# Half of a depthwise conv moved into two MLP blocks, the output projection split by MLP block, and five MLP blocks of 4, 4, 4, 3 and 2 tiles

## The chip, the cores and the metric

The kernel runs on one core of a Trainium2 chip. The metric is the device time of one execution in microseconds (us); three runs of the kernel before gave 2654.08, 2655.58 and 2659.54 us, median 2655.58. Engines: PE is TensorE (matmul; PEld its weight load), DVE is VectorE, ACT is ScalarE, POOL is GpSimd, SP is SyncE, which issues every DMA here. A "tile" of the text is 128 rows of the 17 x 128 = 2176 input rows: tile 0 is the sample rows, tiles 1 to 16 are the prompt.

## The reference, cut to what matters

One layer of an encoder, width 1024, in float32:

```
proj = rmsnorm(x) @ w_in                      # q, k, v, a, g
attn = windowed attention(q, k, v)            # 512 wide; tiles 1..16, and 8 sample batches
u = a * sigmoid(g)                            # 512 channels
c = silu(layernorm(causal depthwise conv of u, 31 taps))
x = x + concat(rmsnorm(attn), rmsnorm(c)) @ w_out
x = x + relu(rmsnorm(x) @ w_up)**2 @ w_down   # 4096 wide
x = x + (p @ w_ple) * sigmoid(rmsnorm(x) @ w_ple_gate);  y = rmsnorm(x)
```

## The kernel before, in words

Every large matmul is done as three, on a high part and a rest of each operand (hi x hi, hi x lo, lo x hi). So each weight of 512 KB is loaded (tile `raw`, 3 buffers), cast on ACT to `w[:, 0]` and its rest taken on POOL to `w[:, 1]` (`weight` and `split`, L117 to L131; weights with a scale take the rest on DVE, L131). There are 8 buffers `w`.

The stages, in order:

- **A**: the columns a and g of `proj`, blocks of 3 tiles; the conv's input goes to `U` (four buffers of 512 prompt rows) and `US` (sample). `conv_block` starts a conv where `CONV_AT` says, 4 tiles at a time. For each of four channel blocks cb it adds 31 taps into an `acc` of 128 x 512: cb 0 to 2 on DVE (L162), cb 3 on POOL (L158) from products of ACT (L157) or POOL (L155). There are 5 buffers `acc`. `conv_post` then does each tile: transposes to PSUM (L168, tile `c`, one buffer), layer norm, back-transposes (L181), swish, store to `M[t]`. Taps have the lowest priority (`LOW`).
- **B**: q, k, v (L266, `mm<-hnb`) and the attention, two or three tiles a block; the result also goes to `M[t]`.
- **C**: `c_tile` loads `M[t]`, splits it and multiplies it with `w_out` (48 matmuls, L533), adds x, and stores `X1[t]`. The eight sample batches are mixed in.
- **MLP**: four blocks of 4, 4, 5 and 4 tiles. A block's normalised, transposed input is `hf` (one buffer; `mlp_front`). The 32 columns f of w_up go in groups of 4: per f 24 matmuls (L266, `up`), then ACT relu and square (L663, L664), DVE `relu<-up,relu` (L665) and the rest `ht<-relu,ht` (L666). After four f come 24 matmuls a tile with w_down (L678, `d`), added to `accf` on DVE (L684). All of w_up and w_down is loaded again for each block.
- **PLE**: the gate with the per-layer embedding, tile by tile.

A scheduler makes each engine's order from priorities and its own idea of time; each engine then runs its list strictly in order. So an instruction that waits holds up all that is behind it on its engine.

Of the kernel before, what the change touches and what calls it, by code (L numbers as in the profile page):

```python
# [72 lines left out]
def build(ctx, tc, nc, a):  # L73
# [64 lines left out]
    cpool = pool(mix, "cpool")
    mixp = ExitStack()
    psc = pool(mixp, "psc", 1, space=PSUM)  # L140

    U = [cpool.tile([P, 4, HALO + 512], F32, name=f"U{i}", bufs=1) for i in range(4)]
    US = cpool.tile([P, 4, DB, HALO + DS], F32, name="US", bufs=1)
    nc.gpsimd.memset(U[0][:, :, 0:HALO], 0.0)

# [18 lines left out]
    def conv_post(accs, off, t):  # L164
        with later(tc, MID):
# [27 lines left out]
            nc.sync.dma_start(M[t][:, 4:8, :], zc)  # L193

    def conv_block(tiles):
        pt = [t for t in tiles if t > 0]
        if 0 in tiles:
            accs = []
            for cb in range(4):
                acc = cpool.tile([P, 512], F32, name="acc", bufs=5)[:, 0:P]  # L200
                accs.append(acc)
                conv_taps(acc.rearrange("p (b s) -> p b s", b=DB),
                          lambda j, cb=cb: US[:, cb, :, j:j + DS], cb,
                          lambda: cpool.tile([P, 512], F32, name="tap")[:, 0:P].rearrange("p (b s) -> p b s", b=DB), 0)
            conv_post(accs, 0, 0)
        if pt:
            n = len(pt) * P
            c0 = (pt[0] - 1) * P
            accs = []
            for cb in range(4):  # L210
                acc = cpool.tile([P, 512], F32, name="acc", bufs=5)
                accs.append(acc)
                conv_taps(acc[:, 0:n], lambda j, cb=cb: U[c0 // 512][:, cb, c0 % 512 + j:c0 % 512 + j + n], cb,
                          lambda: cpool.tile([P, 512], F32, name="tap")[:, 0:n], pt[0])
            for i, t in enumerate(pt):
                conv_post(accs, i * P, t)
# [227 lines left out]
    for bi, tiles in enumerate(B_BLOCKS):  # L444
# [56 lines left out]
        for i in range(nch):  # L501
# [56 lines left out]

    def f_segs(tiles):
        n = len(tiles) * P  # L560
        return [(0, n)] if n <= 512 else [(0, 384), (384, n)]

    def mlp_front(bi, ps, tag, bufs):
        tiles = F_BLOCKS[bi]
        hf = hpool.tile([P, KD, 2, FB * P], F32R, name="hf", align_bytes=ALN)
        hfs[bi] = hf
        xns = []
        for t in tiles:
            xn = hpool.tile([P, D], F32, name="xnf", bufs=XNB)
# [7 lines left out]
    for ti, t in enumerate(C_ORDER[EARLY:]):
        if ti < DB:
            sample_batch(opool, ps2, *samp, ti)
        if ti == DB - 1:  # L580
            nc.sync.dma_start(M[0][:, 0:4, :], samp[2])
        c_tile(t, opool, ps2, opool.tile([P, 8, P], F32, name="mt", bufs=3),
               opool.tile([P, D], F32, name="xc", bufs=3), opool.tile([P, 2, 8, P], F32R, name="ms", bufs=2, align_bytes=ALN),
               opool.tile([P, 8, P], F32, name="sq", bufs=1), dict(bufs=1), dict(bufs=4))
# [56 lines left out]

    for bi, tiles in enumerate(F_BLOCKS):
        segs = f_segs(tiles)
        hf = hfs.pop(bi)
        accs = []
        for t in tiles:
            acc = fpool.tile([P, D], F32, name="accf", bufs=FB)
            nc.sync.dma_start(acc, X1[t])
            accs.append(acc)
        for g in range(NFF // GRP):  # L650
            hts, wds = [], []
            for f in range(g * GRP, (g + 1) * GRP):
                wu = weight(a["w_up"][f].rearrange("p k n -> p (k n)"))
                wd = weight(a["w_down"][f * P:(f + 1) * P, :])
# [3 lines left out]
                for s0, s1 in segs:  # L658
                    w = s1 - s0
                    ps = psf.tile([P, 512], F32, name="up")  # L660
                    proj(ps[:, 0:w], lambda wp, k: wu[:, wp, k * P:(k + 1) * P], lambda k: hf[:, k, :, s0:s1], w)
                    r = fpool.tile([P, 512], F32, name="relu", bufs=2)
                    nc.scalar.activation(r[:, 0:w], ps[:, 0:w], AF.Relu)  # L663
                    nc.scalar.activation(ht[:, 0, s0:s1], r[:, 0:w], AF.Square)  # L664
                    nc.vector.scalar_tensor_tensor(r[:, 0:w], ps[:, 0:w], 0.0, r[:, 0:w], ALU.max, ALU.mult)  # L665
                    nc.vector.tensor_tensor(ht[:, 1, s0:s1], r[:, 0:w], ht[:, 0, s0:s1].bitcast(F32), ALU.subtract)  # L666
            if g == NFF // GRP - 1:
# [20 lines left out]

    def ple_back(t, x2, xg):
        ss = fpool.tile([P, 2], F32, name="gss", bufs=2)  # L690
# [3 lines left out]
        for nh, ns in enumerate((h0, h1)):  # L694
# [119 lines left out]
```

## Time and profile before

| | |
|---|---|
| median of three runs | 2655.58 us |
| profiled execution | 2655.39 us |
| its span, first to last instruction | 2653.6 us |
| mean granted TensorE clock | 0.973 of full speed |
| PE busy | 2526.9 us (95%) |
| DVE busy | 1273.2 us (48%) |
| ACT busy | 978.4 us (37%) |
| POOL busy | 1121.7 us (42%) |
| weight-load DMA of `raw` | 512 KB each, 3.5 us to land |

Read it by stage, not by the totals: stages A and B end at 665 us, the conv's last posts at 689, C at 897, the MLP at 2400, PLE at 2653.6. The 48% of DVE is an average of stages in which it is full and others in which it is a third busy.

### The profile page before, as it was taken

How to read it: one execution, taken by the hardware profiler on the slowest of the kernel's cores; microseconds unless marked ns; L12 is line 12 of the kernel's file. 1: busy time of each engine (PE TensorE's matmuls, PEld its weight loads, DVE VectorE, ACT ScalarE, POOL GpSimd, SP SyncE). 2: the span in 40 equal slices, each digit the busy share in tenths (PEclk: the TensorE clock that was granted, in tenths of full speed). 3: DMA queues.
4: the chain of work that ended last, by engine and by line, in shares of the span. 5: the costliest groups of instructions: out<-in, count | busy, mean ns of one | idle time of the engine just before them, and what ended most of it. 6: DMA issues, size and time to landing. Idle time of an engine off the chain costs nothing.

```text
span 2653.6 us, 32374 instructions
## 1 busy us (share of the span) xinstructions
PE 2526.9 (95%) x12609; PEld 2142.6 (81%) x12609; DVE 1273.2 (48%) x1841; ACT 978.4 (37%) x1889; POOL 1121.7 (42%) x756
## 2 busy tenths in 40 slices
PE   8988597989699999999999999999999999999998
PEld 7888486766588888888888888999999888888887
DVE  7996959796334233234323334334333333344333
ACT  6534366656333322323232333222223322233433
POOL 5534517295344644434443533433233444422221
PEclk9998798989799999999999999999999999999999
DMA  7422331211344533225322334222214323233221
GB/s 234 137 98 88 129 101 45 89 61 60 124 150 154 183 103 102 95 96 175 111 97 94 103 107 148 95 80 73 71 64 154 117 86 105 92 124 121 74 86 40
DMA packets 111257, 283.08 MB, mean 107 GB/s; under 512 B 15360, under 2 KB 47744, under 8 KB 111104
## 3 DMA queue, kind: packets, MB, share of 16 engines
q1 hardware_dynamic: 111104, 281.01, 31.1%
q8 instruction: 99, 1.62, 0.2%
q14 instruction: 54, 0.44, 0.1%
HBM read 226.68 MB, written 54.29 MB: 106 GB/s over the span
## 4 chain that ended last, share of the span: by engine, by line
PE 84%; DVE 12%; POOL 1%; ACT 1%; issue 1%; DMA 1%; SPq 0%; POOLq 0%; ACTq 0%; DVEq 0%
PE up L266 28%; PE d L678 27%; DVE acc L162 9%; PE acc L533 7%; PE pg L699 7%; PE mm L266 7%; PE pq L706 2%; PE o L398 2%; PE s L370 1%; POOL acc L158 1%; PE tr L614 1%; DVE hn L257 0%; PE up L254 0%; DVE mx L345 0%; PE pt L386 0%
## 5 line engine op out<-in xcount | busy, mean ns | idle before, releaser
L118 POOL TENSOR_TENSOR w<-raw,w 128x1024 fp32r<-128x1024 f32 x265 | 643.0, 2442 | 854.3 <-ACT w L117 851.8
L266 PE MATMUL up<-hf,w 128*128 128x512 f32 (+2 forms) x3840 | 757.0, 357 | 0.7 <-DVE hf L257 0.7
L678 PE MATMUL d<-w,ht 128*128 128x512 f32 x3264 | 753.4, 390 | 1.4 <-DVE accf L684 1.4
L266 PEld LDWEIGHTS up<-hf,w 128*128 128x128 f32 x3840 | 658.8, 188 | 91.1 <-DVE hf L257 0.9
L678 PEld LDWEIGHTS d<-w,ht 128*128 128x128 f32 x3264 | 611.2, 188 | 127.7 <-DVE accf L684 1.8
L117 ACT CAST w<-raw 128x1024 fp32r<-128x1024 f32 x266 | 278.5, 1049 | 708.6 <-PE d L678 569.1
L684 DVE TENSOR_TENSOR accf<-d,accf 128x512 f32<-128x512 f32 x272 | 175.2, 686 | 474.8 <-PE d L678 472.2
L162 DVE SCALAR_TENSOR_TENSOR acc<-U,vec,acc 128x512 f32<-128x512 f32 x360 | 345.1, 1006 | 0.4
L665 DVE SCALAR_TENSOR_TENSOR relu<-up,relu 128x512 f32<-128x512 f32 (+2 forms) x160 | 97.7, 611 | 428.5 <-ACT ht L664 428.5
L266 PE MATMUL mm<-hn,w 128*128 128x384 f32 (+1 forms) x1152 | 216.2, 346 | 26.4 <-DVE U L312 13.9
L158 POOL TENSOR_TENSOR acc<-acc,tap 128x512 f32<-128x512 f32 (+1 forms) x150 | 212.8, 1419 | 64.4 <-ACT tap L157 56.5
L666 DVE TENSOR_TENSOR ht<-relu,ht 128x512 fp32r<-128x512 f32 (+2 forms) x160 | 232.5, 1453 | 5.4
L266 PEld LDWEIGHTS mm<-hn,w 128*128 128x128 f32 x1152 | 202.0, 202 | 30.4 <-DVE U L312 15.0
L266 PE MATMUL mm<-hnb,w 128*128 128x256 f32 (+1 forms) x1152 | 190.4, 316 | 35.3 <-DMA hnb<-H 14.0
L266 PEld LDWEIGHTS mm<-hnb,w 128*128 128x128 f32 x1152 | 165.5, 203 | 59.5 <-issue 25.6
L663 ACT ACTIVATE relu<-up 128x512 f32<-128x512 f32 (+2 forms) x160 | 85.3, 533 | 300.7 <-PE up L266 298.6
L533 PE MATMUL acc<-w,ms 128*128 128x512 f32 x768 | 188.5, 400 | 1.0 <-ACT ms L117 1.0
L533 PEld LDWEIGHTS acc<-w,ms 128*128 128x128 f32 x768 | 143.1, 190 | 31.0 <-ACT ms L117 1.3
L699 PE MATMUL pg<-wgh,xg 128*128 128x512 f32 x408 | 99.5, 393 | 0.0
L699 PE MATMUL pg<-w,xg 128*128 128x512 f32 x408 | 98.4, 390 | 0.0
L664 ACT ACTIVATE ht<-relu 128x512 fp32r<-128x512 f32 (+2 forms) x160 | 90.5, 566 | 1.9
L537 DVE SCALAR_TENSOR_TENSOR xc<-acc,ors,xc 128x512 f32<-128x512 f32 x64 | 47.8, 750 | 89.3 <-PE acc L533 65.8
(176 smaller groups left out, 2037.4 us busy)
## 6 DMA issues: line engine op xcount, KB each, us to landing
raw<-in_w_up SPq DMA_DIRECT2D x128, 512.0 KB, 3.5
raw<-in_w_down SPq DMA_DIRECT2D x128, 512.0 KB, 3.5
H<-hn SPq DMA_DIRECT2D x20, 768.0 KB, 4.4
hnb<-H SPq DMA_DIRECT2D x56, 256.0 KB, 4.3
xt<-in_x SPq DMA_DIRECT2D x17, 512.0 KB, 5.9
xnf<-X SPq DMA_DIRECT2D x17, 512.0 KB, 5.9
accf<-X SPq DMA_DIRECT2D x17, 512.0 KB, 5.4
X<-accf SPq DMA_DIRECT2D x17, 512.0 KB, 3.5
```

Of the source, the lines that this page charges most:

```text
L117: nc.scalar.copy(hi, src)
L118: (eng or nc.gpsimd).tensor_tensor(lo, src, hi.bitcast(F32), ALU.subtract)
L158: nc.gpsimd.tensor_tensor(acc, acc, t, ALU.add)
L162: nc.vector.scalar_tensor_tensor(acc, view(j), cw[:, j, cb:cb + 1], acc, ALU.mult, ALU.add)
L266: nc.tensor.matmul(ps, w(wp, k), m[:, ap_, 0:n], start=(i == 0), stop=(i == 3 * KD - 1))
L533: nc.tensor.matmul(ps, ms[:, ap_, k, :], wo[k][:, wp, nh * 512:(nh + 1) * 512], start=(i == 0), stop=(i == 11))
L664: nc.scalar.activation(ht[:, 0, s0:s1], r[:, 0:w], AF.Square)
L665: nc.vector.scalar_tensor_tensor(r[:, 0:w], ps[:, 0:w], 0.0, r[:, 0:w], ALU.max, ALU.mult)
L666: nc.vector.tensor_tensor(ht[:, 1, s0:s1], r[:, 0:w], ht[:, 0, s0:s1].bitcast(F32), ALU.subtract)
L678: nc.tensor.matmul(pd[nh], hts[f][:, hp, i * P:(i + 1) * P], wds[f][:, wp, nh * 512:(nh + 1) * 512], start=(j == 0), stop=(j == 3 * GRP - 1))
L684: nc.vector.tensor_tensor(xs, pd[nh], xs, ALU.add)
L699: nc.tensor.matmul(pg, xg[ap_][:, k * P:(k + 1) * P], wg[k][:, wp, ns], start=(i == 0), stop=(i == 3 * KD - 1))
```

## The change

- The convs of tiles 9 to 12 and 13 to 16 leave stages A and B. `conv_late` does them inside MLP blocks 0 and 1: two taps (of all four cb) are traced behind each of the first f of the block, after that f's `relu<-up,relu` and square and before its `ht<-relu,ht`.
- Stage C keeps tile 1 (in B), 2, 3 and 4 and the sample batches. The output projection of the other 13 tiles is `c_late`, traced before the last f group of the MLP block ahead of the one that uses them; `load_wo` loads w_out again each time.
- The MLP blocks are [1-4], [5-8], [9-12], [13-15], [16, 0], so w_up and w_down are loaded five times. In the last two blocks some w_down rests go to DVE.
- PSUM: `up` has 3 buffers where it had 4; the tile `c` of the posts keeps one for the whole kernel.

The core of the diff:

```
-CONV_AT = {0: [0], 1: [1, 2, 3, 4], 2: [5, 6, 7, 8], 4: [9, 10, 11, 12], 5: [13, 14, 15, 16]}
+CONV_AT = {0: [0], 1: [1, 2, 3, 4], 2: [5, 6, 7, 8]}
+CONV_LATE = {0: [9, 10, 11, 12], 1: [13, 14, 15, 16]}
+LATE_TAPS = 2
-F_BLOCKS = [[1, 2, 3, 4], [5, 6, 7, 8], [9, 10, 11, 12, 0], [13, 14, 15, 16]]
+F_BLOCKS = [[1, 2, 3, 4], [5, 6, 7, 8], [9, 10, 11, 12], [13, 14, 15], [16, 0]]
+    def conv_late(pt):
...
+        accs = [cpool.tile([P, 512], F32, name="acc", bufs=5) for _ in range(4)]
+        for j in range(KC):
+            for cb in range(4):
...
+                if cb in PCB:
...
+                        nc.scalar.activation(t, v, AF.Copy, scale=w_)
+                        nc.gpsimd.tensor_tensor(acc, acc, t, ALU.add)
...
+                    nc.vector.scalar_tensor_tensor(acc, v, w_, acc, ALU.mult, ALU.add)
+            yield
+        for i, t in enumerate(pt):
+            conv_post(accs, i * P, t)
+            yield
...
+    def c_late(t):
+        mt = hpool.tile([P, 8, P], F32, name="mtl", tag="xnf", bufs=XNB)
+        xt = hpool.tile([P, D], F32, name="xcl", tag="xnf", bufs=XNB)
+        nc.sync.dma_start(mt, M[t])
...
+            split(m[:, 0], m[:, 1], mt[:, 4 * h:4 * h + 4])
...
+                        nc.tensor.matmul(pd[nh], ms[h][:, ap_, k, :], wo[4 * h + k][:, wp, nh * 512:(nh + 1) * 512],
+                                         start=(i == 0), stop=(i == 11))
...
+                nc.vector.scalar_tensor_tensor(xs, pd[nh], rs[:, h:h + 1], xs, ALU.mult, ALU.add)
+        nc.sync.dma_start(X1[t], xt)
...
+            last = g == NFF // GRP - 1
+            if last and bi + 1 < len(F_BLOCKS):
+                load_wo()
+                for t in F_BLOCKS[bi + 1]:
+                    c_late(t)
...
+                wd = weight(a["w_down"][f * P:(f + 1) * P, :], None, nc.vector if f % 4 >= len(tiles) else None)
...
+                sq = nc.scalar.activation(ht[:, 0, 0:n], r[:, 0:n], AF.Square)
+                hs = nc.vector.scalar_tensor_tensor(r[:, 0:n], ps[:, 0:n], 0.0, r[:, 0:n], ALU.max, ALU.mult)
+                with later(tc, LOW), tc.issue_after(sq.ins), tc.issue_after(hs.ins):
+                    for _ in range(LATE_TAPS):
+                        next(late, None)
+                nc.vector.tensor_tensor(ht[:, 1, 0:n], r[:, 0:n], ht[:, 0, 0:n].bitcast(F32), ALU.subtract)
```

PE, end of stage B and start of C. Before (`sp` is a sample batch, `c` a conv post, `acc<-w,ms` the output projection):

```order
L398 MATMUL o<-p_6525,va 128x512
L398 MATMUL o<-p_6532,va 128x512
L181 MATMUL c<-ident,z 128x128 x4
L414 MATMUL sp<-ident,vtn 16x128 x8
L168 MATMUL c<-ident,acc 128x128 x4
```

Three such pairs of `c` follow before the first batch. In the changed kernel:

```order
L424 MATMUL o<-p_5912,va 128x512
L424 MATMUL o<-p_5919,va 128x512
L440 MATMUL sp<-ident,vtn 16x128 x8
L447 MATMUL sp<-ks,qb 128x144
L452 MATMUL sp<-ident,pr 128x128
```

The posts of tiles 13 to 16 have left this place.

DVE in MLP block 0 of the changed kernel, from one f to the end of a group of four f (`U_139` is the buffer of tiles 9 to 12):

```order
L736 SCALAR_TENSOR_TENSOR relu<-up,relu 128x512
L215 SCALAR_TENSOR_TENSOR acc<-U_139,vec,acc 128x512 x3
L740 TENSOR_TENSOR ht<-relu,ht 128x512
L215 SCALAR_TENSOR_TENSOR acc<-U_139,vec,acc 128x512 x3
L758 TENSOR_TENSOR accf<-d,accf 128x512 x8
```

The first four rows stand four times in a group; before, a group was `relu<-up,relu` and `ht<-relu,ht` four times and then the `accf`. Each rest now has 3 taps ahead of it and 3 behind it on DVE. On POOL the eight rests of weights of such a group now stand among eight `acc<-acc,tap`, five and six of them within the four f.

PE at the end of MLP block 1 of the changed kernel (`c` posts of tiles 9 to 12, `accl` the output projection of tiles 9 and 10):

```order
L182 MATMUL c<-ident,z 128x128
L752 MATMUL d<-w,ht 128x512 x48
L169 MATMUL c<-ident,acc 128x128 x4
L653 MATMUL accl<-w,msl 128x512 x33
L643 MATMUL stl<-ones,sql 128x1 x2
L653 MATMUL accl<-w,msl 128x512 x15
L182 MATMUL c<-ident,z 128x128 x4
L169 MATMUL c<-ident,acc 128x128 x4
L182 MATMUL c<-ident,z 128x128 x4
L169 MATMUL c<-ident,acc 128x128 x4
L653 MATMUL accl<-w,msl 128x512 x35
```

The posts of block 0's conv stand here, a block later, and between two projections. And DVE at this place (`U_140` is the buffer of tiles 13 to 16):

```order
L186 TENSOR_SCALAR zc<-c,half 128x128 x4
L213 TENSOR_SCALAR acc<-U_140,vec 128x512 x2
L215 SCALAR_TENSOR_TENSOR acc<-U_140,vec,acc 128x512
L172 BN_STATS st<-c 128x6
L215 SCALAR_TENSOR_TENSOR acc<-U_140,vec,acc 128x512 x2
L193 SCALAR_TENSOR_TENSOR zc<-th,zc 128x512
L173 BN_AGGR mv<-st 128x2
L215 SCALAR_TENSOR_TENSOR acc<-U_140,vec,acc 128x512 x8
```

With five `acc` and four of them held by the posts of tiles 9 to 12, cb 1 and 2 of tiles 13 to 16 start only here: 62 of the 93 taps on DVE stand from this place on, among the `xcl<-accl` that empty the projection's PSUM, and before the last group's `relu<-up,relu`.

## Rows read from the trace of the kernel before

**Rows 1.** Windows: start:end, us, busy us (count) of PE PEld DVE ACT POOL, clock, DMA.
```profile
277.00:350.00 73.00, 50.75 (x290) 48.47 (x291) 68.54 (x85) 25.16 (x62) 33.74 (x22) 0.81 0.35 117
350.00:400.00 50.00, 49.19 (x333) 39.16 (x332) 23.69 (x58) 36.49 (x116) 11.65 (x14) 1.00 0.37 121
400.00:475.00 75.00, 61.55 (x347) 48.22 (x347) 75.00 (x101) 46.71 (x130) 51.92 (x29) 0.86 0.13 43
475.00:525.00 50.00, 49.83 (x309) 37.06 (x307) 32.49 (x87) 36.48 (x122) 4.24 (x8) 1.00 0.24 78
525.00:600.00 75.00, 68.00 (x382) 51.30 (x379) 74.60 (x107) 36.10 (x112) 68.42 (x40) 0.89 0.24 81
...
608.00:665.00 57.00, 52.85 (x238) 30.31 (x236) 30.49 (x75) 37.84 (x132) 37.16 (x32) 1.00 0.12 43
665.00:689.00 24.00, 7.98 (x37) 5.10 (x36) 10.63 (x29) 5.96 (x11) 2.22 (x6) 0.60 0.11 44
689.00:698.00 9.00, 3.16 (x9) 1.83 (x9) 1.65 (x7) 2.77 (x9) 0.11 (x1) 0.50 0.65 238
698.00:897.00 199.00, 199.00 (x929) 164.12 (x930) 73.22 (x137) 65.19 (x123) 95.79 (x96) 0.99 0.38 140
897.00:2400.00 1503.00, 1500.98 (x7219) 1282.22 (x7218) 548.10 (x646) 450.74 (x626) 619.72 (x263) 1.00 0.32 109
```

**Rows 2.** Windows of tile `acc` alone: busy us (count) of PE PEld DVE POOL.
```profile
400.00:475.00 75.00, 0.27 (x1) 0.14 (x1) 61.77 (x65) 48.05 (x27) 0.86 0.13 43
```

**Rows 3.** Chain in order of time around the conv's last posts: start, us, engine, line.
```profile
671.48 1.13 PE c L181 x4
672.63 1.38 DVE zc L185 x4
...
674.77 0.69 DVE zc L192
...
678.42 1.13 PE c L181 x4
...
691.89 4.85 DMA mt<-M
696.77 1.05 ACT ms L117
```

**Rows 4.** Chain in the MLP: 4-tile groups, and one of the 5-tile block.
```profile
851.95 11.01 PE acc L533 x48
...
1117.40 19.04 PE up L266 x84
1136.44 10.88 PE d L678 x48
...
1602.30 28.40 PE up L266 x192
```

**Rows 5.** Timeline, DVE, POOL and ACT: start, us, engine, line, operation, count, idle before.
```profile
269.62 2.06 DVE L162 SCALAR_TENSOR_TENSOR acc<-U,vec,acc 128x512 f32<-128x512 f32 x3
280.31 20.30 POOL L158 TENSOR_TENSOR acc<-acc,tap 128x512 f32<-128x512 f32 x12 [1.61 <-ACT tap L157]
287.67 13.49 DVE L162 SCALAR_TENSOR_TENSOR acc<-U,vec,acc 128x512 f32<-128x512 f32 x8
...
1001.91 0.63 ACT L664 ACTIVATE ht<-relu 128x512 fp32r<-128x512 f32 x1
1002.08 2.40 POOL L118 TENSOR_TENSOR w<-raw,w 128x1024 fp32r<-128x1024 f32 x1 [3.04 <-ACT w L117]
1002.57 0.69 DVE L665 SCALAR_TENSOR_TENSOR relu<-up,relu 128x512 f32<-128x512 f32 x1 [2.98 <-ACT ht L664]
1003.30 1.74 DVE L666 TENSOR_TENSOR ht<-relu,ht 128x512 fp32r<-128x512 f32 x1
...
2381.68 0.68 DVE L666 TENSOR_TENSOR ht<-relu,ht 128x512 fp32r<-128x512 f32 x1
```

**Rows 6.** DMA issues: tile, queue, count, KB each, median us to landing.
```profile
M<-zc SPq DMA_DIRECT2D x17, 256.0 KB, 2.0
```

More of the change, by code (lines that the diff above doesn't have):

```diff
@@ L132, in weight @@
         return w
+    cpool = pool(ctx, "cpool")
+    psc = pool(ctx, "psc", 1, space=PSUM)
     mix = ExitStack()
[L138 to L143, printed above, removed]
+    upool = pool(mix, "upool", 1)
+    U = [(upool if i < 2 else cpool).tile([P, 4, HALO + 512], F32, name=f"U{i}", bufs=1) for i in range(4)]
+    US = upool.tile([P, 4, DB, HALO + DS], F32, name="US", bufs=1)
     nc.gpsimd.memset(U[0][:, :, 0:HALO], 0.0)
@@ L193, in conv_post @@
             nc.sync.dma_start(M[t][:, 4:8, :], zc)
+    def conv_late(pt):
+        n = len(pt) * P
+        c0 = (pt[0] - 1) * P
+        accs = [cpool.tile([P, 512], F32, name="acc", bufs=5) for _ in range(4)]
+        for j in range(KC):
+            for cb in range(4):
+                v = U[c0 // 512][:, cb, c0 % 512 + j:c0 % 512 + j + n]
+                w_, acc = cw[:, j, cb:cb + 1], accs[cb][:, 0:n]
+                if cb in PCB:
+                    if j == 0:
+                        nc.gpsimd.tensor_scalar(acc, v, w_, g_b[:, cb:cb + 1], ALU.mult, ALU.add)
+                    else:
+                        t = cpool.tile([P, 512], F32, name="tap", align_bytes=ALN)[:, 0:n]
+                        nc.scalar.activation(t, v, AF.Copy, scale=w_)
+                        nc.gpsimd.tensor_tensor(acc, acc, t, ALU.add)
+                elif j == 0:
+                    nc.vector.tensor_scalar(acc, v, w_, g_b[:, cb:cb + 1], ALU.mult, ALU.add)
+                else:
+                    nc.vector.scalar_tensor_tensor(acc, v, w_, acc, ALU.mult, ALU.add)
[3 more added lines that the diff above has]
+            yield
     def conv_block(tiles):
@@ L203, in conv_block @@
                           lambda j, cb=cb: US[:, cb, :, j:j + DS], cb,
-                          lambda: cpool.tile([P, 512], F32, name="tap")[:, 0:P].rearrange("p (b s) -> p b s", b=DB), 0)
+                          lambda: cpool.tile([P, 512], F32, name="tap", align_bytes=ALN)[:, 0:P].rearrange("p (b s) -> p b s", b=DB), 0)
             conv_post(accs, 0, 0)
@@ L213, in conv_block @@
                 conv_taps(acc[:, 0:n], lambda j, cb=cb: U[c0 // 512][:, cb, c0 % 512 + j:c0 % 512 + j + n], cb,
-                          lambda: cpool.tile([P, 512], F32, name="tap")[:, 0:n], pt[0])
+                          lambda: cpool.tile([P, 512], F32, name="tap", align_bytes=ALN)[:, 0:n], pt[0])
             for i, t in enumerate(pt):
@@ L506, in build, with load_wo @@
                 nc.sync.dma_start(M[1 + (c0 + i) // 2][:, 0:4, :], mta)
-    wo = []
-    with later(tc, -PREO):
+    wo = [None] * KD
+    def load_wo():
         for k in range(KD):
             g = g_attn[:, k:k + 1] if k < 4 else g_conv[:, k - 4:k - 3]
-            wo.append(weight(a["w_out"][k * P:(k + 1) * P, :], g))
+            wo[k] = weight(a["w_out"][k * P:(k + 1) * P, :], g)
+    with later(tc, -PREO):
+        load_wo()
     def c_tile(t, pl, ps_, mt, xt, ms, sq, stt, acct):
@@ L572, in mlp_front @@
             xns.append(xn)
-        for s0, s1 in f_segs(tiles):
-            transpose_split(lambda k: hf[:, k, :, s0:s1], xns[s0 // P:s1 // P], g_ffn, ps, tag, bufs)
+        transpose_split(lambda k: hf[:, k, :, 0:len(tiles) * P], xns, g_ffn, ps, tag, bufs)
     samp = sample_start(opool, ps2)
[L577 to L583, printed above, removed]
+    sb = 0
+    for ti, t in enumerate(F_BLOCKS[0][EARLY:]):
+        for _ in range(3):
+            if sb < DB:
+                sample_batch(opool, ps2, *samp, sb)
+                sb += 1
+        c_tile(t, opool, ps2, hpool.tile([P, 8, P], F32, name="mt", tag="xnf", bufs=XNB),
+               hpool.tile([P, D], F32, name="xc", tag="xnf", bufs=XNB),
+               opool.tile([P, 2, 8, P], F32R, name="ms", bufs=1, align_bytes=ALN),
                opool.tile([P, 8, P], F32, name="sq", bufs=1), dict(bufs=1), dict(bufs=4))
-        if ti == FRONT0:
-            mlp_front(0, ps2, "sp", 2)
+    mlp_front(0, ps2, "sp", 2)
+    nc.sync.dma_start(M[0][:, 0:4, :], samp[2])
     pc.close()
     psmp.close()
-    mixp.close()
     pf = ExitStack()
@@ L596, in build, with up_ps @@
     psf = pool(pf, "psf", 4, space=PSUM)
+    def up_ps(name):
+        return psf.tile([P, 512], F32, name=name, tag="up", bufs=UPB)
+    def c_late(t):
+        mt = hpool.tile([P, 8, P], F32, name="mtl", tag="xnf", bufs=XNB)
+        xt = hpool.tile([P, D], F32, name="xcl", tag="xnf", bufs=XNB)
+        nc.sync.dma_start(mt, M[t])
+        nc.sync.dma_start(xt, a["x"][t])
+        st = up_ps("stl")
+        ms = []
+        for h in range(2):
+            m = fpool.tile([P, 2, 4, P], F32R, name="msl", tag="ht", bufs=GRP + 2, align_bytes=ALN)
+            split(m[:, 0], m[:, 1], mt[:, 4 * h:4 * h + 4])
+            ms.append(m)
+            sq = fpool.tile([P, 4, P], F32, name="sql", tag="relu", bufs=2)
+            nc.scalar.activation(sq, mt[:, 4 * h:4 * h + 4], AF.Square)
+            nc.gpsimd.tensor_tensor(sq[:, 0:2], sq[:, 0:2], sq[:, 2:4], ALU.add)
+            nc.gpsimd.tensor_tensor(sq[:, 0], sq[:, 0], sq[:, 1], ALU.add)
+            nc.tensor.matmul(st[:, h:h + 1], sq[:, 0], ones[:, 0:1], start=True, stop=True)
+        rs = fpool.tile([P, 2], F32, name="orl", bufs=2)
+        nc.vector.tensor_scalar(rs, st[:, 0:2], 1.0 / CC, EPS, ALU.mult, ALU.add)
+        nc.gpsimd.tensor_tensor(rs, rs, mhalf, ALU.pow)
+        for h in range(2):
+            pd = [psf.tile([P, 512], F32, name="accl", tag="d") for _ in range(2)]
+            i = 0
+            for k in range(4):
+                for ap_, wp in ((0, 0), (0, 1), (1, 0)):
+                    for nh in range(2):
+                        nc.tensor.matmul(pd[nh], ms[h][:, ap_, k, :], wo[4 * h + k][:, wp, nh * 512:(nh + 1) * 512],
+                                         start=(i == 0), stop=(i == 11))
+                    i += 1
+            for nh in range(2):
+                xs = xt[:, nh * 512:(nh + 1) * 512]
+                nc.vector.scalar_tensor_tensor(xs, pd[nh], rs[:, h:h + 1], xs, ALU.mult, ALU.add)
+        nc.sync.dma_start(X1[t], xt)
+        ss = fpool.tile([P, 1], F32, name="osl", bufs=2)
+        nc.scalar.activation(mt.rearrange("p k n -> p (k n)"), xt, AF.Square, accum_out=ss)
+        rstd(rs1[:, t:t + 1], ss, 1.0 / D)
     def ple_front(t):
@@ L600, in ple_front @@
         nc.sync.dma_start(x2, X2[t])
-        pe = fpool.tile([P, PLE], F32, name="pe", bufs=3)
+        pe = cpool.tile([P, PLE], F32, name="pe", tag="acc", bufs=5)
         nc.sync.dma_start(pe, a["pt"][t])
@@ L608, in ple_front @@
         nc.vector.tensor_scalar(xn, x2, rs, None, ALU.mult)
-        xg = [fpool.tile([P, 10 * P], F32R, name="xg", tag="ht", bufs=GRP + 2, align_bytes=ALN) for _ in range(2)]
-        split(xg[0][:, 8 * P:10 * P], xg[1][:, 8 * P:10 * P], pe)
+        xg = [fpool.tile([P, D], F32R, name="xg", tag="ht", bufs=GRP + 2, align_bytes=ALN) for _ in range(2)]
+        xp = cpool.tile([P, 2, PLE], F32R, name="xp", tag="tap", align_bytes=ALN)
+        split(xp[:, 0], xp[:, 1], pe)
         for q, nk in ((0, 4), (4, 4)):
-            tp = psf.tile([P, 512], F32, name="tr", tag="up")
+            tp = up_ps("tr")
             for i in range(nk):
@@ L642, in build @@
     for bi, tiles in enumerate(F_BLOCKS):
-        segs = f_segs(tiles)
+        n = len(tiles) * P
         hf = hfs.pop(bi)
@@ L657, in build @@
                 hts.append(ht)
[L658 to L667, printed above, removed]
+                ps = up_ps("up")
+                proj(ps[:, 0:n], lambda wp, k: wu[:, wp, k * P:(k + 1) * P], lambda k: hf[:, k], n)
+                r = fpool.tile([P, 512], F32, name="relu", bufs=2)
+                nc.scalar.activation(r[:, 0:n], ps[:, 0:n], AF.Relu)
+                sq = nc.scalar.activation(ht[:, 0, 0:n], r[:, 0:n], AF.Square)
[4 more added lines that the diff above has]
+                nc.vector.tensor_tensor(ht[:, 1, 0:n], r[:, 0:n], ht[:, 0, 0:n].bitcast(F32), ALU.subtract)
+            if last:
                 if bi + 1 < len(F_BLOCKS):
-                    mlp_front(bi + 1, psf, "up", 4)
+                    mlp_front(bi + 1, psf, "up", UPB)
                 else:
```

31 lines of the change are left out of this document (14 added, 17 removed).

## The prediction, made before the changed kernel ran

> **What bounds the kernel now.** I read the windows by stage first, then the chain of waits, then the timeline for single durations.
>
> From 897 us on PE is busy without a gap at full clock [rows 1]: the MLP is bound by PE alone, 19.04 us for 84 matmuls, 0.2267 us each [rows 4]. Adding work to DVE, ACT or POOL there is free only while PE never waits for it. Stage B is different. Where the conv's taps fill DVE (400 to 475 and 525 to 600 us, DVE 75.0 and 74.6 of 75 us), PE does 347 and 382 matmuls in 75 us; where they don't (350 to 400, 475 to 525), 333 and 309 in 50 us; the clock is at 1.00 in the light stretches and 0.86 to 0.89 in the full ones [rows 1]. So DVE holds up B. Behind the attention stand 24 us (665 to 689) in which PE is busy 8 us: the posts of the last four tiles, one after the other, 6.94 us apart (671.48 to 678.42) [rows 1, 3]. Stage C is then PE bound again, with 11.0 us for the 48 matmuls of a tile [rows 4].
>
> The sum is made against the profiled execution: 2655.39 us, span 2653.6; the median of the runs is 2655.58, so both are one number here.
>
> **What the change takes away.** 186 taps on DVE and 62 on cb 3, and eight posts, leave A and B.
> - Heavy windows of B: the light ones do 642 matmuls in 100 us, 6.42 per us; the 729 of the heavy ones at that rate need 113.6 us instead of 150: 36 us. At least 20 (the mix is not equal), at most 41 (all at the 6.66 per us of 350 to 400).
> - 277 to 350 us: 290 matmuls in 73 us with DVE full for 68.5 [rows 1]. At 6.42 per us they would take 45, but most are wider here, and taps of tiles 1 to 8 stay: 15, between 0 and 28.
> - Attention tail, 608 to 665 us: 57 us, PE 52.9 [rows 1]. A little of it moves forward: 8, between 0 and 15.
> - The four posts: 24, and PE's order shows them gone. What is late next is the first sample batch, as before (689 to 698).
> Gain 83, between 44 and 108.
>
> **What is only moved.** Stage C with the batch ahead of it takes 208 us now (689 to 897). PE's matmuls are the same in number and width: the 5-tile block was already cut into 3 and 2. Of C, 13 tiles go to the MLP: 13 x 11.1 = 144 us. What stays: 9 us until the first projection, three tiles (33), the batches' own matmuls among them (6), the last three batches, which now have nothing beside them (an estimate of 5 us each, from a post's period of 6.94, whose chain is a little longer: 14), and the transposes for `hf`, eight steps of one DVE pass of 0.69 and a little (8): about 70. Together 214, a loss of 6.
>
> The 64 more weights and 32 loads of w_out hide beside PE: POOL works 620 of 1503 us in the MLP, ACT 451 [rows 1].
>
> **What is added: waits of PE in the MLP.** Five places.
>
> (1) *The four groups of block 0 with taps.* By DVE's order, between the first `relu` product of a group and the rest of its fourth f stand 4 products, 4 rests and 21 taps. Alone a tap takes 0.687 (2.06 for 3), a rest 0.68, a product 0.69 [rows 5]: 2.8 + 2.7 + 14.4 = 19.9 us. PE needs the fourth rest after 72 further matmuls of `up` and 22 of `d`, 94 x 0.2267 = 21.3, less some 1.3 for relu and square ahead of the first product: 20.0. So with no disturbance it fits exactly, and every us by which POOL holds DVE up is a wait of PE. POOL does hold it: beside POOL's run of adds eight taps took 13.49, 1.69 each, the time of one tap and one add (POOL's own 20.30 / 12 = 1.69), and a rest that began during POOL's 2.40 us took 1.74 and ended 0.56 after it [rows 5]. In that stretch of a group POOL has five rests of weights (2.40) and some six adds (1.69 - 0.69 = 1.0): 18 us. From 400 to 475, 65 taps took 61.8 us, 17 more than 65 x 0.687, beside 27 adds of 1.0: 63% of POOL's time came through [rows 2]. That makes 11.3 a group, 45 in all; between 0 and 4 x 18 = 72. During the rest of the group DVE has only `accf`, but the next taps stand behind a product that PE has not made, so they cannot use it.
>
> The Trainium skill says of this (SBUF — State Buffer, Who interferes with whom) that a DVE instruction with two SBUF inputs and a GpSimd instruction that reads SBUF exclude each other, the second waiting for the whole of the first. The 1.69 agrees. By that rule taken to its end place (1) costs the 72; without it, nothing.
>
> (2) *The end of block 1.* Here PE's list has the posts of tiles 9 to 12, which the projection of these tiles needs. The first projection waits for `M[9]`: swish, store 2.0, load 4.85, split, some 4 us beyond the matmuls beside it [rows 3, 6]. Then two more back-transposes stand before tile 10's matmuls, one post period apart: 14 us with no work for PE. From there DVE has 62 to 64 taps with 14 additions of the projection (as long as a product) between them, and only behind them the products of the last group: at 0.687 a tap 55 us, at the 0.95 of [rows 2] 74, at 1.69 more than 110, against 44 of PE's work. Late by 11, 30 or 64. Sum 14 + 30 = 44, between 25 and 78.
>
> (3) *The 2-tile block.* A group of PE is 96 matmuls of 256 columns (28.40 us for 192 of 384 and 256 mixed [rows 4] makes about 0.12 each) and 48 of 512: 22.4 us for 8 weights, 2.8 each; POOL has six of 2.40, which fits, but four buffers `w` are held until the last `d`, and the fourth w_up then comes about 2 us late: 15, between 0 and 30.
>
> (4) *The end of block 2.* Posts of tiles 13 to 16, three of which the next block needs; tile 13's way from its back-transpose through `M` (1.38 + swish 0.6 and 0.69 + store 2.0 + load 4.85 + split 1.05 and a rest of about 1.2 [rows 3, 6]) is 12 us beside no ready projection: 16, between 8 and 28.
>
> (5) *The other ends.* Block 0 (tiles 5 to 8 are ready long before): 4. Block 3, where tile 16's last back-transpose has 5.4 us of `d` behind it and 12 us of way: 6. The start of PLE, whose weights have 10.9 us of `d` to hide behind instead of 21.8: 3. Sum 13, between 3 and 30.
>
> Waits: 45 + 44 + 15 + 16 + 13 = 133, between about 40 and 230. Total 2655.4 - 83 + 6 + 133 = **2711 us**, 2.1% slower.
>
> **Rivals.**
> - *The MLP absorbs it* (faster). POOL's rests fall where DVE waits for PE anyway, so place (1) costs 10, and the taps at the end of block 1 run at 0.687. Then the waits are 10 + 25 + 5 + 10 + 5 = 55 and the time is 2655 - 83 + 6 + 55 = 2633. For it: in the MLP of before DVE works 548 us of 1503 [rows 1], so there is room on the average. Against: the taps are not spread over that room, and the 1.74 of a rest beside POOL is the state of the MLP now.
> - *The port between DVE and POOL decides* (much slower). The exclusion is full in (1), 72, and at the end of block 1 the taps take 1.69: 78; with 30, 28 and 25 elsewhere the time is 2655 - 60 + 6 + 233 = 2834. It decides from the point at which POOL always has an instruction ready when DVE ends one. Against: 37% of POOL's time did not come through at 400 to 475, so half of the way, say 2770, is likelier. (The rule of the Trainium skill's page SBUF — State Buffer, Who interferes with whom, is this rival without slack; the 1.74 agrees with it.)
> - *The change doesn't do what it says.* For block 1 this is so by the order: two thirds of the taps on DVE run at the block's end. It is in (2). If the end is crossed at no cost, because DVE overtakes there, 44 become 14, and the time is 2681.
> - *Gains and waits cancel*: 2655, if the heavy windows give 50 and more and (1) stays at 20.
>
> **How the numbers follow.** Forecast (waits of 90 to 175 us, time 2670 to 2755): 0.55. MLP absorbs: 0.25. Port decides: 0.15. Cancel, within 0.2% (about what a measurement here can tell from no change, 5 us): 0.05. Faster by over 0.2%: 0.25 and a little of the third rival's and the cancelling case's edge: 0.26. Within: 0.04. Slower: 0.70. The range of 8 in 10 must reach into both neighbours: 2600 to 2790; the likeliest case's own is 2670 to 2755.
>
> **What would show it.** Right: B's matmuls at more than 6 per us up to the end of the attention; no posts behind it; C over some 70 us after its first batch; in block 0 groups with taps of about 55 us and groups without of 43.5; in those, PE's `d` waiting for `ht<-relu,ht` of DVE; taps on DVE over 0.9 us; PE gaps at the end of block 1 of 30 us and more, for `c` and `accl`, with DVE full; groups of the 2-tile block of 23 to 25 us. Wrong: groups of block 0 at 43.5 to 47 us (then (1) is false), or block ends without gaps (then (2) and (4)), or B no faster than now (then the first part of the gain).

## The result, and the profile after

The changed kernel takes 2744.14 us (median of four runs, 2742.71 to 2746.31) against 2656.52 us before: a ratio of 1.033, 95% interval 1.0312 to 1.0348. The profiled execution has a span of 2741.9 us, 88.3 more than before. The forecast was 2711 us, slower; the direction and most places are right, the sum is 33 us short of the median.

Windows by stage of the changed kernel (us, then busy time and count of PE, PEld, DVE, ACT, POOL, granted clock, DMA share, GB/s), against [rows 1]:

```profile
277.00:350.00 73.00, 60.17 (x345) 53.82 (x346) 53.82 (x75) 36.44 (x101) 34.35 (x25) 0.88 0.35 115
350.00:614.40 264.40, 261.79 (x1566) 192.28 (x1564) 78.03 (x229) 166.22 (x551) 12.05 (x16) 1.00 0.25 82
614.40:697.60 83.20, 63.10 (x269) 47.25 (x268) 39.36 (x74) 35.34 (x88) 36.07 (x26) 0.79 0.48 171
697.60:934.80 237.20, 200.28 (x790) 161.19 (x791) 170.74 (x157) 69.17 (x94) 126.11 (x61) 0.89 0.21 73
1404.00:1606.50 202.50, 164.12 (x702) 132.11 (x701) 151.06 (x167) 79.18 (x111) 129.38 (x90) 0.89 0.36 123
1856.80:2009.00 152.20, 141.58 (x641) 116.48 (x640) 66.95 (x97) 56.26 (x76) 64.59 (x53) 0.96 0.44 151
2308.00:2487.00 179.00, 179.00 (x1155) 163.76 (x1154) 123.10 (x123) 92.59 (x136) 109.38 (x48) 1.00 0.61 200
```

Stage B is nearly what was forecast: from 350 us to the end of the attention PE is busy 261.8 of 264.4 us at full clock, and the attention ends at 614.4 instead of 665. The MLP starts at 697.6. There the time is given back: in the tap groups of block 0 (to 934.8), at the end of block 1 (1404 to 1606) and at that of block 2 (1857 to 2009). The 2-tile block (2308 to 2487) has PE busy throughout.

One group of block 0 with taps, PE in order of time (start, us; in brackets idle time before and what ended it):

```profile
807.54 11.04 PE L752 MATMUL d<-w,ht 128*128 128x512 f32 x48
818.42 17.16 PE L292 MATMUL up<-hf,w 128*128 128x512 f32 x75
835.42 2.43 PE L752 MATMUL d<-w,ht 128*128 128x512 f32 x10
842.69 4.83 PE L752 MATMUL d<-w,ht 128*128 128x512 f32 x11 [4.84 <-DVE ht L740]
852.48 7.80 PE L752 MATMUL d<-w,ht 128*128 128x512 f32 x23 [4.95 <-DVE ht L740]
...
876.66 17.16 PE L292 MATMUL up<-hf,w 128*128 128x512 f32 x75
```

From 818.42 to 876.66 are 58.2 us, where a group without taps takes 43.5. Two waits of 4.9 us are for `ht` of DVE; the other 4.9 of the 14.7 is matmuls that run slower behind a wait (11 in 4.83 us instead of 2.5, 23 in 7.80 instead of 5.4). The granted clock is 1.00 up to the first wait, 0.54 from 842.7 to 847.5 and 0.68 from 852.5 to 860.2 (means of its two levels, half and full speed). DVE and POOL in the same stretch:

```profile
820.60 0.69 DVE L736 SCALAR_TENSOR_TENSOR relu<-up,relu 128x512 f32<-128x512 f32 x1 [0.91 <-ACT ht L735]
821.21 6.68 DVE L215 SCALAR_TENSOR_TENSOR acc<-U,vec,acc 128x512 f32<-128x512 f32 x3
827.82 1.78 DVE L740 TENSOR_TENSOR ht<-relu,ht 128x512 fp32r<-128x512 f32 x1
829.52 7.40 DVE L215 SCALAR_TENSOR_TENSOR acc<-U,vec,acc 128x512 f32<-128x512 f32 x3
836.85 0.68 DVE L736 SCALAR_TENSOR_TENSOR relu<-up,relu 128x512 f32<-128x512 f32 x1
...
842.56 2.07 DVE L215 SCALAR_TENSOR_TENSOR acc<-U,vec,acc 128x512 f32<-128x512 f32 x3
...
857.94 0.68 DVE L740 TENSOR_TENSOR ht<-relu,ht 128x512 fp32r<-128x512 f32 x1
```

```profile
815.67 7.13 POOL L119 TENSOR_TENSOR w<-raw,w 128x1024 fp32r<-128x1024 f32 x3 [20.56 <-ACT w L118]
822.77 1.75 POOL L211 TENSOR_TENSOR acc<-acc,tap 128x512 f32<-128x512 f32 x1
824.48 2.87 POOL L119 TENSOR_TENSOR w<-raw,w 128x1024 fp32r<-128x1024 f32 x1
827.30 1.75 POOL L211 TENSOR_TENSOR acc<-acc,tap 128x512 f32<-128x512 f32 x1
829.01 5.65 POOL L119 TENSOR_TENSOR w<-raw,w 128x1024 fp32r<-128x1024 f32 x2
834.63 1.75 POOL L211 TENSOR_TENSOR acc<-acc,tap 128x512 f32<-128x512 f32 x1
836.33 2.82 POOL L119 TENSOR_TENSOR w<-raw,w 128x1024 fp32r<-128x1024 f32 x1
...
844.34 2.52 POOL L119 TENSOR_TENSOR w<-raw,w 128x1024 fp32r<-128x1024 f32 x1 [3.52 <-ACT w L118]
```

Three taps take 6.68 or 7.40 us while POOL works without a pause, and 2.07 at 842.56, where POOL is idle up to 844.34. `relu<-up,relu`, which has one of its two inputs in PSUM, takes its usual 0.68 beside POOL's rest at 836.33. The idle 20.56 us ahead of POOL's row at 815.67 matter most below. POOL has nothing to do beside `d`: ACT's casts, which come before its rests, wait for buffers that `d` still reads, as the page of the changed kernel has it (of 669 us of idle time, 488 ended by `d`):

```profile
L118 ACT CAST w<-raw 128x1024 fp32r<-128x1024 f32 x330 | 345.3, 1049 | 669.2 <-PE d L752 488.4
```

Then POOL does the eight rests of a group between 815.67 and 846.86, most of them beside `up`.

The end of block 1, PE; the first row shows a post of tiles 9 to 12 standing behind the `d` of the block's last group but one, the second-last a wait for the projection's addition:

```profile
1458.68 0.60 PE L169 MATMUL c<-ident,acc 128*128 128x128 f32 x4
...
1477.36 1.12 PE L182 MATMUL c<-ident,z 128*128 128x128 f32 x4 [3.47 <-ACT z L179]
...
1508.65 0.48 PE L169 MATMUL c<-ident,acc 128*128 128x128 f32 x1 [9.28 <-DVE zc L186]
...
1533.78 4.55 PE L653 MATMUL accl<-w,msl 128*128 128x512 f32 x13 [3.91 <-DVE xcl L658]
...
1563.32 2.21 PE L752 MATMUL d<-w,ht 128*128 128x512 f32 x4 [10.67 <-DVE xcl L658]
...
1606.55 21.92 PE L292 MATMUL up<-hf,w 128*128 128x512 f32 x96
```

That addition stands on DVE behind eight taps:

```profile
1549.84 12.68 DVE L215 SCALAR_TENSOR_TENSOR acc<-U,vec,acc 128x512 f32<-128x512 f32 x8
1562.43 1.40 DVE L658 SCALAR_TENSOR_TENSOR xcl<-accl,orl,xcl 128x512 f32<-128x512 f32 x2
```

### The profile page after: what moved, and what is told of

The parts are those of the page before. It is cut to its first block, busy times and chain, and to the rows that moved or that the text cites. A ratio compares the mean times of both kernels' runs of the same rounds, so it can differ in the third digit from the quotient of the medians.

```text
span 2741.9 us, 33002 instructions
## 1 busy us (share of the span) xinstructions
PE 2556.0 (93%) x12609; PEld 2152.8 (79%) x12609; DVE 1433.0 (52%) x1897; ACT 1103.9 (40%) x2041; POOL 1195.6 (44%) x805
## 4 chain that ended last, share of the span: by engine, by line
PE 81%; DVE 15%; DMA 1%; issue 1%; ACT 1%; POOL 1%; SPq 0%; POOLq 0%; ACTq 0%; DVEq 0%
PE d L752 26%; PE up L292 24%; PE mm L292 8%; PE pg L773 7%; DVE acc L215 6%; DVE acc L163 5%; PE accl L653 4%; PE o L424 2%; PE pq L780 2%; PE s L396 2%; PE acc L563 1%; DVE ht L740 1%; PE pt L412 1%; PE pt L418 1%; PE tr L681 1%
## 5 line engine op out<-in xcount | busy, mean ns | idle before, releaser
L119 POOL TENSOR_TENSOR w<-raw,w 128x1024 fp32r<-128x1024 f32 x305 | 756.1, 2495 | 673.6 <-ACT w L118 668.0
L752 PE MATMUL d<-w,ht 128*128 128x512 f32 x3264 | 780.2, 397 | 49.0 <-DVE ht L740 38.0
L752 PEld LDWEIGHTS d<-w,ht 128*128 128x128 f32 x3264 | 621.2, 192 | 183.4 <-DVE ht L740 42.3
L118 ACT CAST w<-raw 128x1024 fp32r<-128x1024 f32 x330 | 345.3, 1049 | 669.2 <-PE d L752 488.4
L215 DVE SCALAR_TENSOR_TENSOR acc<-U,vec,acc 128x512 f32<-128x512 f32 x180 | 244.4, 1402 | 0.0
L163 DVE SCALAR_TENSOR_TENSOR acc<-U,vec,acc 128x512 f32<-128x512 f32 x180 | 185.5, 1084 | 0.3
L653 PE MATMUL accl<-w,msl 128*128 128x512 f32 x624 | 158.0, 413 | 13.2 <-ACT msl L118 8.1
L653 PEld LDWEIGHTS accl<-w,msl 128*128 128x128 f32 x624 | 123.2, 200 | 40.8 <-ACT msl L118 9.5
L159 POOL TENSOR_TENSOR acc<-acc,tap 128x512 f32<-128x512 f32 (+1 forms) x90 | 115.2, 1281 | 44.5 <-ACT tap L158 38.0
L773 PE MATMUL pg<-w,xg 128*128 128x512 f32 x510 | 125.4, 392 | 0.0
L773 PEld LDWEIGHTS pg<-w,xg 128*128 128x128 f32 x510 | 94.6, 188 | 18.8
```

Of the source, the lines that this page charges most:

```text
L118: nc.scalar.copy(hi, src)
L119: (eng or nc.gpsimd).tensor_tensor(lo, src, hi.bitcast(F32), ALU.subtract)
L159: nc.gpsimd.tensor_tensor(acc, acc, t, ALU.add)
L163: nc.vector.scalar_tensor_tensor(acc, view(j), cw[:, j, cb:cb + 1], acc, ALU.mult, ALU.add)
L215: nc.vector.scalar_tensor_tensor(acc, v, w_, acc, ALU.mult, ALU.add)
L653: nc.tensor.matmul(pd[nh], ms[h][:, ap_, k, :], wo[4 * h + k][:, wp, nh * 512:(nh + 1) * 512], start=(i == 0), stop=(i == 11))
```

## The experiments

The theory: the late taps cost because DVE's taps and POOL's work shut each other out, and the taps stand where POOL does its rests. The main rival: DVE simply has too many instructions per group. Ratios are against the kernel before, timed beside them (2654.96 us for runs 1 to 4, 2652.64 for runs 5 to 8), with 95% intervals. What a group takes is the steady distance from one group to the next; without taps it is 43.5 us.

**1. The conv back in A and B, the rest of the change kept** (label conv_in_b).

```
-CONV_AT = {0: [0], 1: [1, 2, 3, 4], 2: [5, 6, 7, 8]}
-CONV_LATE = {0: [9, 10, 11, 12], 1: [13, 14, 15, 16]}
+CONV_AT = {0: [0], 1: [1, 2, 3, 4], 2: [5, 6, 7, 8], 4: [9, 10, 11, 12], 5: [13, 14, 15, 16]}
+CONV_LATE = {}
```

> Undoes one part: the whole conv is traced in stages A and B as before, while the projection per block and the blocks of 4, 4, 4, 3 and 2 stay. Theory (the late conv costs the waits in block 0, at the end of block 1 and of block 2, 63 + 46 + 10; the block-wise projection itself costs little): those waits go, and so do the 50 us that the attention gained and the 22 us of posts behind it: 2744 - 119 + 73, about 2695 (2680 to 2705). Rival (the projection and the weights of w_out at each block's end cost the time): the ends of blocks keep gaps of 15 us and more without the conv, and the time is 2730 or above.

Measured: 2663.62 us, ratio 1.003 (1.0018 to 1.0041); 16 us less than the lowest that was expected. Block-wise projection and five blocks cost some 8 us; the late conv costs the other 80. The end of the attention and the start of the MLP, PE:

```profile
671.72 0.66 PE L182 MATMUL c<-ident,z 128*128 128x128 f32 x4
672.22 1.04 PE L440 MATMUL sp<-ident,vtn 128*16 128x128 f32 x8
673.84 0.66 PE L169 MATMUL c<-ident,acc 128*128 128x128 f32 x4 [0.59 <-DVE zc L186]
675.18 0.51 PE L447 MATMUL sp<-ks,qb 128*128 128x144 f32 x2 [0.68 <-ACT vn L441]
...
753.79 6.49 PE L292 MATMUL up<-hf,w 128*128 128x512 f32 x19 [0.71 <-DVE hf L283]
```

The posts that stood alone before the first sample batch [rows 3] now run beside it. So this run is the right one to set the change against, and it splits the 88 us of the span: up to the first `up` the late conv gains 753.8 - 697.6 = 56; from there to the end it costs 2044.3 - 1908.1 = 136; the rest of the change costs 8 (before: 1756.7 from the first `up`, and 13 tiles of 11.04 moved there, 1900).

**2. Posts of the late conv ranked ahead** (posts_early).

```
-            conv_post(accs, i * P, t)
+            conv_post(accs, i * P, t, -LOW)      # priority in place of MID
```

> The posts of the late conv are ranked ahead of the MLP's work instead of behind it, so that they run as soon as their taps are done; the taps stay two per f. Theory (an MLP group has no room for 24 taps on DVE, wherever they stand): the buffers of the second conv come free at the start of block 1, so four groups of block 1 now take 58 us as those of block 0 do (4 x 14.8 = 59 us more), while the gap at the end of block 1 (about 50 us) falls to about 4 and that of block 2 (13.5) to about 4: sum 59 - 46 - 10, the time stays at 2735 to 2755. Rival (only the place of the posts costs, the taps would hide): the two gaps go and block 1's groups stay near 43.5 to 46: 2685 to 2700.

Measured: 2728.08 us, ratio 1.027 (1.0254 to 1.0285), 7 us below the expected range, but with the pattern of the theory: the ends of blocks 1 and 2 take what they take in the run without the late conv (in both 91.4 and 79.2 us from the last addition to `accf` of the seventh group to that of the eighth), and the groups at the start of block 1 now take 58 us. The wait moved; it did not go.

```profile
1221.31 17.16 PE L292 MATMUL up<-hf,w 128*128 128x512 f32 x75
...
1245.56 4.99 PE L752 MATMUL d<-w,ht 128*128 128x512 f32 x11 [4.82 <-DVE ht L740]
```

**3. One tap per f, over twice as many groups** (thin_posts; posts as in 2).

```
-LATE_TAPS = 2
+LATE_TAPS = 1       # and one conv_late behind the other, over blocks 0 to 2
```

> One tap per f instead of two, the second conv following the first without regard to blocks (70 steps over 96 f's), posts ranked ahead as in the run with early posts. Theory (a group has room for some 20 us on DVE; 12 taps at 1.4 and eight passes of the MLP fit nearly): the 17 groups with taps take 44.5 to 47 us, the ends of blocks 1 and 2 have gaps below 6: 2744 - 63 - 46 - 10 + 17 x 1 to 3, that is 2642 to 2676. Rival (every tap ahead of a rest costs the same, however thinly they are spread): 17 x 7.4 = 126 us of waits instead of 63 and the ends' gaps gone: 2745 to 2755.

Measured: 2731.27 us, ratio 1.0278 (1.0261 to 1.0295). My expectation failed: groups with 12 taps take 51.2 us, 7.7 more than without, so 17 groups cost about as much as eight of 14.7. It was not a matter of room on DVE. In such a group:

```profile
808.32 6.68 DVE L215 SCALAR_TENSOR_TENSOR acc<-U,vec,acc 128x512 f32<-128x512 f32 x3
...
818.32 6.80 DVE L215 SCALAR_TENSOR_TENSOR acc<-U,vec,acc 128x512 f32<-128x512 f32 x3
```

With half the taps, the first six still take 13.5 us: POOL's rests, which they meet, are as many as before. The rival's price for a group (7.4) came, its time (2745 to 2755) did not. That a tap costs the same wherever it stands is tested by 6.

**4. Without POOL's adds** (no_adds): the products and adds of cb 3 in the late conv left out.

```
-                    else:
+                    elif False:
                         t = cpool.tile([P, 512], F32, name="tap", ...)
```

> Leaves out taps 2 to 31 of channel block 3 in the late conv: ACT's products and POOL's adds for it are gone, DVE's own list of taps is as it was. Theory (POOL's instructions hold DVE's up): POOL's adds, some 6 of its 18 us in the stretch that counts, no longer stand in the way, so the tap groups fall from 58.3 to 51 to 54, late taps from 1.40 us to about 1.1, the gap at the end of block 1 from 50 to 25 to 35: 2744 - 20 - 20, about 2700. Rival (it is the number of DVE instructions alone, POOL is beside the point): groups stay at 58, taps at 1.4: 2740. Second rival (the exclusion is without slack and the weights' rests alone fill it): groups 55 and 2725.

Measured: 2706.33 us, ratio 1.0193 (1.0178 to 1.0208), groups of 50 to 51, late taps 1.19 us on the mean. The direction of the theory; but the end of block 1 lost only 9 us (193.4 for 202.4), less than expected. PE's idle time there fell from 38 to 30 us.

**5. Without POOL's rests** (no_rests; on top of 2).

```
-            split(w[:, 0], w[:, 1], raw, lo_eng)
+            nc.scalar.copy(w[:, 0], raw)         # blocks 0 and 1 only
+            nc.scalar.copy(w[:, 1], raw)
```

> As the run with early posts, but in blocks 0 and 1 ACT writes both halves of a weight as casts, so that the low half is not the rest but a second cast, and POOL has nothing of the weights. Theory: the 24 taps beside up meet only POOL's adds, some six a group: taps about 0.9 us, groups 45 to 50 instead of 57: 2728 less 9 groups times 7 to 12, 2620 to 2665. Rival (POOL is beside the point): groups 57, 2728. ACT has 8 more casts of 1.05 a group, which may cost a few us of its own.

Measured: 2627.05 us, ratio 0.99 (0.9883 to 0.9916), 101 us less than run 2 with the same taps in the same places: groups of 43.4 to 45.1 in block 0. So the main rival is out, since DVE has as many instructions as in run 2. DVE and then POOL at one place:

```profile
806.49 4.15 DVE L219 SCALAR_TENSOR_TENSOR acc<-U,vec,acc 128x512 f32<-128x512 f32 x3
...
822.50 2.06 DVE L219 SCALAR_TENSOR_TENSOR acc<-U,vec,acc 128x512 f32<-128x512 f32 x3
```

```profile
806.60 3.49 POOL L215 TENSOR_TENSOR acc<-acc,tap 128x512 f32<-128x512 f32 x2 [12.83 <-ACT tap L214]
```

Three taps beside two adds take 4.15 us. Alone three taps take 2.06, and an add 1.26 (the kernel before, at 640.14 us): in sum 4.58. So the two engines work almost one at a time, some 0.2 us a pair less than the sum; side by side they would have needed 2.5.

**6. The same taps beside `d`** (taps_beside_d): as many a group as in run 3, one conv behind the other as there, but all of them behind the rests `ht` of the group. They no longer rank behind the MLP's work.

```
+                with tc.issue_after(sq.ins), tc.issue_after(hs.ins):   # hs: last ht or accf
+                    for _ in range(LATE_TAPS):                         # 1, ahead of each tile's d
+                        next(late, None)
                 pd = [psf...
```

> One tap (of all four channel blocks) ahead of each tile's d instead of behind each f's product: 12 DVE taps a group, all between the rest of the group's last f and its last addition to accf; one conv behind the other, posts where their turn comes. The runs before showed that 12 taps ahead of the rests cost as much each as 24 do, so room on DVE isn't the matter. Theory (a DVE tap and a POOL instruction shut each other out; POOL's rests of weights stand in one row beside up and POOL idles beside d): here taps take 0.7 to 0.9 us, and groups 43.5 to 45: 2655 - 54 + 8 + 17 x 0.7, 2610 to 2630, faster than before. Rival (a tap costs about 0.55 us of PE wherever it stands): groups of 50 and 2731, as with one tap per f.

Measured: 2617.68 us, ratio 0.9865 (0.985 to 0.988): faster than both kernels, as expected. A group with taps and no post takes 43.5 us, and from 702.1 to 1630 us PE never waits. The taps and POOL's rests in one group:

```profile
783.79 2.07 DVE L215 SCALAR_TENSOR_TENSOR acc<-U,vec,acc 128x512 f32<-128x512 f32 x3
...
789.82 2.06 DVE L215 SCALAR_TENSOR_TENSOR acc<-U,vec,acc 128x512 f32<-128x512 f32 x3
...
817.81 5.20 DVE L215 SCALAR_TENSOR_TENSOR acc<-U,vec,acc 128x512 f32<-128x512 f32 x3
```

```profile
791.33 15.12 POOL L119 TENSOR_TENSOR w<-raw,w 128x1024 fp32r<-128x1024 f32 x6 [10.69 <-ACT w L118]
...
817.29 6.87 POOL L211 TENSOR_TENSOR acc<-acc,tap 128x512 f32<-128x512 f32 x4
```

Three of the four sets of taps run at 0.69 each in POOL's idle time; the one that meets POOL's four adds takes 5.20, and `d` covers it.

**7. Two taps ahead of each tile's `d`** (taps24_beside_d): the edit of 6 with `LATE_TAPS = 2`, each conv in its own block.

> The same place with two taps ahead of each tile's d, so 24 a group, in nine groups of blocks 0 and 1 each. Theory: 24 x 0.69 + 8 x 0.68 = 22 us against 21.8 of d, a little more where POOL's adds or first rests meet them: groups of 44 to 48, 2620 to 2650. Rival (the number of taps a group decides): 57 a group as with early posts, 2728.

Measured: 2685.51 us, ratio 1.0118 (1.0103 to 1.0133), groups of 49 to 54: better than 58 with as many taps beside `up`, but missed by 35 us. I had counted 0.69 a tap; now POOL's eight adds of a group come in a row beside its first taps (the last row below shows seven, its window ends at 840 us), and its rests begin 3 us into the last fourteen taps:

```profile
793.96 11.84 DVE L215 SCALAR_TENSOR_TENSOR acc<-U,vec,acc 128x512 f32<-128x512 f32 x8
...
806.91 9.30 DVE L215 SCALAR_TENSOR_TENSOR acc<-U,vec,acc 128x512 f32<-128x512 f32 x6
...
829.70 10.30 DVE L215 SCALAR_TENSOR_TENSOR acc<-U,vec,acc 128x512 f32<-128x512 f32 x6
```

```profile
796.91 16.76 POOL L119 TENSOR_TENSOR w<-raw,w 128x1024 fp32r<-128x1024 f32 x6 [5.95 <-ACT w L118]
...
829.17 11.97 POOL L211 TENSOR_TENSOR acc<-acc,tap 128x512 f32<-128x512 f32 x7
```

**8. Each f's rest ahead of its taps** (rest_first): the changed kernel with the line of `ht<-relu,ht` moved up.

> The kernel after the change, but the six taps of an f stand behind its rest instead of three ahead and three behind; number and half of the group are the same. Theory (what counts is that taps and POOL's rests fall into the same 23 us): the last rest then stands behind 18 taps instead of 21, groups 55 to 58, 2730 to 2744. Rival (a rest must not stand behind its own f's taps): d waits no longer, groups 44 to 46, 2685 to 2695.

Measured: 2742.88 us, ratio 1.0339 (1.0323 to 1.0354): no change, groups of 57 to 58. The order within an f does not matter.

## Why the prediction was right, and where its sum was off

- *Stage B.* 36 + 15 + 8 = 59 us were forecast for the heavy windows, 277 to 350 and the tail. The attention ends at 614.4 instead of 665, 51 us earlier; against run 1, where it ends at 671.8, it is 57. Nearly right: with 1566 matmuls in 264.4 us PE does 5.9 a us, where more than 6 was named as the sign.
- *The four posts and stage C.* 24 us of gain and 6 of loss were forecast, 18 together. From the end of the attention to the first `up` the kernel before has 232 us, less the 144 that moved 88; the changed kernel has 83: 5 came. Against run 1, which has 82, it is nothing: with the conv in B the posts run beside the first sample batch there and add no time. The step that failed is "what stays: about 70": the last three batches have long waits for ACT (3.3 and 2.7 us, at 670.11 and 676.80) and the clock is at 0.79. The 24 were a property of the old order more than of the conv.
- *(1) The tap groups.* 45 forecast; 56 measured (279.9 us from the first `up` to the end of the fifth group, against 223.6 in run 1). The mechanism is the one that was named: without POOL's rests the taps nearly fit (run 5, groups of 43.4 to 45.1), as the sum 19.9 against 20.0 said, and what POOL does comes on top. Two parts of the sum were off and partly cancel. From the first product (820.60) to the end of the fourth rest (858.62) DVE takes 38.0 us, not 19.9: 18 us more, where 11.3 were forecast. Six rests and eight adds of POOL fall into this stretch, not five and six, and at the prediction's prices 81% of their 22 us came through, not the 63% of stage B. But PE does 44 matmuls of `d` ahead of the four that need this rest (in run 5 it waits for DVE ahead of these four), not 22: 5 us more work to hide behind. So the rest comes 13 us late for PE. The remainder of the 14.7 is the lower clock, for which the sum had no term. That taps "cannot use" the rest of the group was right for their place in the order, and run 6 shows what that place was worth.
- *(2) The end of block 1.* 44 forecast; 55 measured (1404.13 to 1606.55, 202.4 us, against 147.0 between the same two places of run 1). PE is idle for 38 of them, 20 ahead of matmuls of the posts (14 forecast) and 18 for other results of DVE, which stand behind taps (30 forecast); the other 17 are matmuls that run slower, granted clock 0.89 against 1.00 in run 1, and the sum had nothing for them. Run 2 shows that the posts' place in PE's list makes it: it holds the buffers `acc`, and with them the second conv, until the block's end.
- *(3) and (5).* 15 + 13 forecast; 14 measured. (3) came to nothing: the 2-tile groups take 22.4 us, as their matmuls do alone, so the weights are not late. The 14 are 8 in run 1 for the rest of the change and 6 more at block 3's end.
- *(4) The end of block 2.* 16 forecast; 17.5 measured (152.3 against 134.8).

So the waits were 143 for 133, the gain 56 for 77: of the 88 us of the span the forecast had 56, and two thirds of what it lacks lie in the gain, most of that in the posts and stage C. That the waits came so near is in part luck: (3) was 15 too much, and the clock was left out. The rival in which the MLP absorbs the taps is false for this order of instructions; it is nearly true for the order of run 6. The rival of the port had 72 and 78 us for (1) and (2), farther from the 56 and 55 than the forecast, and its own time (2834) was too long: the taps outlast POOL's rests and then run at 0.69. But the 18 us a group by which it held up DVE in (1) came, and its mechanism is the one that the runs show, with a little slack: 4.15 us in run 5, where the sum is 4.58. The prediction read 1.69 us as the time of one tap and one add; alone they take 1.95, so the slack was there too. The Trainium skill's rule for this (SBUF — State Buffer, Who interferes with whom) is that a DVE instruction with two SBUF inputs and a GpSimd instruction that reads SBUF exclude each other for the whole of an instruction. Run 5 agrees with it but for that slack.

Not settled: why the end of block 1 gained only 9 us in run 4.

## What to carry to other kernels

Free time of an engine is not enough to hide work on it: ask what the neighbour on the same memory does in that very stretch. Here 12 taps a group cost 7.7 us beside `up`, where POOL took its rests, and nothing beside `d`, where POOL mostly waited for buffers. Thinning the work out or changing its order within the busy stretch moved nothing; moving it by half a group gave 114 us (2617.7 against 2731.3).

## What the runs showed that was not expected

- POOL's rests come in a burst behind a pause: all eight of a group in 31 us among its adds, after 20.6 us without work, in the changed kernel; six in a row of 15 us, after 10.7, in run 6. The casts ahead of them wait for buffers that `d` still reads. POOL's 44% on the page hides this.
- Taps and POOL's instructions nearly add up: 4.15 us for three taps and two adds that take 2.06 and 2 x 1.26 alone. The one kind of DVE instruction there with an input in PSUM was not held up: `relu<-up,relu` took 0.68 beside a rest of POOL, `ht<-relu,ht` 1.74 [rows 5].
- A late tap's mean time was 1.40 us in the changed kernel, 1.59 with half as many a group (run 3), 1.19 without the adds, 1.05 without the rests, and 1.03 beside `d` with both.
- Slower matmuls are part of what a wait costs: PE is busy for 2556.0 us against 2526.9 before, with the same 12609 matmuls.
